# MLP up projection as Strassen products through DRAM, and the down projection as a phase of its own

## The chip, the cores and the metric

The kernel runs on one core of a Trainium2 chip. The metric is the device time of one execution in microseconds (us). The engines are PE (TensorE: matmuls and transposes), DVE (VectorE), ACT (ScalarE), POOL (GpSimd) and SP (SyncE, which here only issues DMAs). Each engine works through its own list of instructions in order.

## The reference

One encoder layer on 1024 tokens with a model width of 1024, and a final norm: windowed attention and a bidirectional SSD side by side, merged by gates, then cross attention, then the MLP with a hidden width of 4096. The change concerns the end:

```python
h = rmsnorm(x, norm_cross[i])
x = x + cross_attention(h, rmsnorm(mem, norm_mem[i]), w_xq[i], w_xkv[i], w_xo[i])
h = rmsnorm(x, norm_ffn[i])
x = x + jnp.square(jax.nn.relu(h @ w_up[i])) @ w_down[i]
return rmsnorm(x, norm_final)
```

All values are float32. A product is taken with each factor split in two parts, `hi` (rounded) and `lo` (the rest), and as three matmuls: hi by hi, hi by lo, lo by hi.

## The kernel before

A scheduler gives each engine its order from the program and from estimated durations; the order of the work is then fixed, and instructions wait on semaphores. Tiles come from pools in rotation: a tag has so many buffers, and who asks for the next waits until its last user is done.

`split_in` (L59 to L68) loads 128x1024 weights into `raw`, ACT writes their `hi` (L67) and POOL their `lo` (L68). `wload` gives it three buffers of each kind. `mm3` (L82, L86, L87) issues the three matmuls of a product. `gemm_fm` computes 128 hidden columns for 512 tokens: 8 slices of the width by 3 matmuls of 128x512. `norm_tile` (L130) norms 128 tokens (ACT L128, DVE L119, POOL L121, DVE L136), transposes them on PE (L141) and splits them into the tiles `kt` (ACT L144, DVE L145).

At the end of `merge_cross_phase` the cross attention's output projection, `xo_units`, adds 128x256 results (`xops`) into the eight residual tiles `x1` (L762), which stay in SBUF. For the second half of the tokens its four column groups alternate with the norms of the first half; the norms of the second half follow.

`mlp_phase` has 16 blocks of two hidden tiles of 128. `up` computes both tiles for both halves of the tokens into PSUM (`ups`, 96 matmuls in a block), forms relu(v) * v (ACT L822, DVE L824) and splits it (ACT L826, DVE L827) into `u`; it also loads the down weights (`wdh`, `wdl`). The down projection of a block adds, for eight token tiles and two column halves, six matmuls (`dps`) and one addition to `x1` (L850). The up projection of the next block is asked for ahead of the down projection of this one, so that both are mixed on PE. PSUM has four buffers of one bank (tag `p`: `xops`, `nt`, `dps`) and two of two banks (tag `g`: `ups`). The last block norms each token tile after its second addition and stores it (L854, L855).

## Time and profile before

| what | value |
|---|---|
| time, median of 3 runs (lowest to highest) | 2539.83 us (2535.67 to 2540.74) |
| span of the profiled execution | 2540.5 us |
| PE busy | 2446.7 us, 96% of the span |
| DVE, ACT, POOL busy | 1286.9, 1030.6, 936.2 us |
| matmuls of up and down projection | 1536 and 1536, of 128x512 |
| DMA traffic | 212.20 MB, 84 GB/s in the mean |

The span runs from the first to the last instruction of the profiled execution; that execution has no time of its own beside it, and the span lies 0.7 us over the median of the timed runs. Up and down projection take the last 700 us. "Busy" of PE counts matmuls that overlap in the array, so that a matmul's own duration is longer than the distance to the next one.

### The profile page before, as it was taken

What the parts mean: (1) busy time and instruction counts of PE and PEld (TensorE: products, weight loads), DVE (VectorE), ACT (ScalarE), POOL (GpSimd) and SP (SyncE); (2) the same over time, 40 slices, a digit from 0 to 9 for tenths busy, and PEclk for the clock granted to TensorE, in tenths of its full rate; (3) what the DMA queues carried; (4) which work ended last, traced back from release to release, by engine and by line L of the source; (5) the groups of instructions that cost most, each with busy time, mean ns of one, the idle gap of its engine ahead of it and who ended that gap; (6) DMA issues with size and microseconds to landing.
All of it is one profiled execution on the core that took longest, in us unless ns stands there. A gap on an engine that the chain in (4) does not pass through costs nothing.

```text
span 2540.5 us, 32272 instructions
## 1 busy us (share of the span) xinstructions
PE 2446.7 (96%) x12348; PEld 2014.4 (79%) x12348; DVE 1286.9 (51%) x2033; ACT 1030.6 (41%) x2114; POOL 936.2 (37%) x808
## 2 busy tenths in 40 slices
PE   7899999999999999999999999999999999999998
PEld 6677877777787778777778878888988888888887
DVE  5856556565755655465553342335543434343435
ACT  5445436363544534576773232235432121212112
POOL 4253434344344433444454444224332131312120
PEclk9999999999999999999999999999999999999999
DMA  6223223131313312111125454412121121111111
GB/s 221 75 71 104 92 59 117 52 123 46 112 63 88 108 44 90 48 48 46 50 90 201 134 206 129 170 50 67 59 75 67 34 67 34 66 34 58 42 34 67
DMA packets 135914, 212.20 MB, mean 84 GB/s; under 512 B 9680, under 2 KB 84560, under 8 KB 135760
## 3 DMA queue, kind: packets, MB, share of 16 engines
q1 hardware_dynamic: 58528, 159.80, 18.9%
q10 hardware_dynamic: 77232, 50.35, 6.7%
q8 instruction: 97, 1.59, 0.3%
q14 instruction: 57, 0.47, 0.1%
HBM read 183.63 MB, written 26.48 MB: 83 GB/s over the span
## 4 chain that ended last, share of the span: by engine, by line
PE 71%; DVE 12%; ACT 6%; POOL 4%; DMA 3%; issue 3%; ACTq 0%; POOLq 0%; SPq 0%; DVEq 0%
PE dps L87 4%; PE dps L86 4%; PE dps L82 4%; PE ups L82 4%; PE ups L86 4%; PE ups L87 4%; PE mps L87 3%; PE mps L82 3%; PE mps L86 3%; PE zp L82 2%; PE zp L87 2%; PE zp L86 2%; DMA rows<-d_cs 2%; PE st L373 2%; PE gps L82 2%
## 5 line engine op out<-in xcount | busy, mean ns | idle before, releaser
L68 POOL TENSOR_TENSOR wlo<-raw,whi 128x1024 fp32r<-128x1024 f32 x170 | 416.6, 2452 | 570.4 <-ACT whi L67 556.4
L67 ACT ACTIVATE whi<-raw 128x1024 fp32r<-128x1024 f32 x172 | 181.8, 1057 | 365.0 <-PE mps L86 111.7
L850 DVE TENSOR_TENSOR x<-x,dps 128x512 f32<-128x512 f32 x256 | 175.6, 686 | 124.9 <-PE dps L87 123.2
L68 POOL TENSOR_TENSOR wdl<-raw,wdh 128x1024 fp32r<-128x1024 f32 x32 | 76.0, 2396 | 423.2 <-ACT wdh L67 423.2
L82 PE MATMUL cps<-kt,whi 128*128 128x512 f32 x512 | 203.0, 396 | 6.9 <-DVE cx L334 6.9
L86 PE MATMUL cps<-kt,whi 128*128 128x512 f32 x512 | 203.8, 398 | 0.0
L87 PE MATMUL cps<-kt,wlo 128*128 128x512 f32 x512 | 201.4, 393 | 0.0
L82 PE MATMUL ups<-kt,whi 128*128 128x512 f32 x512 | 199.7, 390 | 0.2
L86 PE MATMUL ups<-kt,whi 128*128 128x512 f32 x512 | 199.4, 390 | 0.0
L87 PE MATMUL ups<-kt,wlo 128*128 128x512 f32 x512 | 199.2, 389 | 0.0
L86 PE MATMUL dps<-wdl,u 128*128 128x512 f32 x512 | 199.2, 389 | 0.0
L87 PE MATMUL dps<-wdh,u 128*128 128x512 f32 x512 | 199.2, 389 | 0.0
L82 PE MATMUL dps<-wdh,u 128*128 128x512 f32 x512 | 199.2, 389 | 0.0
L824 DVE TENSOR_TENSOR u<-ups,ru 128x512 f32<-128x512 f32 x64 | 44.1, 689 | 256.5 <-ACT ru L822 254.3
L67 ACT ACTIVATE wdh<-raw 128x1024 fp32r<-128x1024 f32 x32 | 32.3, 1053 | 229.9 <-PE dps L87 229.7
L82 PEld LDWEIGHTS cps<-kt,whi 128*128 128x128 f32 x512 | 96.6, 189 | 27.1 <-issue 7.7
L82 PEld LDWEIGHTS ups<-kt,whi 128*128 128x128 f32 x512 | 96.1, 188 | 20.7 <-DVE u L824 0.6
L86 PEld LDWEIGHTS ups<-kt,whi 128*128 128x128 f32 x512 | 96.1, 188 | 20.0 <-DVE kt L145 0.2
L87 PEld LDWEIGHTS ups<-kt,wlo 128*128 128x128 f32 x512 | 96.1, 188 | 20.0
L87 PEld LDWEIGHTS dps<-wdh,u 128*128 128x128 f32 x512 | 96.1, 188 | 20.0
L82 PEld LDWEIGHTS dps<-wdh,u 128*128 128x128 f32 x512 | 96.1, 188 | 20.0
L86 PEld LDWEIGHTS dps<-wdl,u 128*128 128x128 f32 x512 | 96.1, 188 | 19.9
(311 smaller groups left out, 6460.2 us busy)
## 6 DMA issues: line engine op xcount, KB each, us to landing
rows<-d_cs ACTq DMA_DIRECT2D x128, 256.0 KB, 3.8
raw<-in_wssd_dram SPq DMA_DIRECT2D x48, 512.0 KB, 3.9
raw<-in_wsb_dram SPq DMA_DIRECT2D x32, 512.0 KB, 3.3
raw<-in_wup_dram SPq DMA_DIRECT2D x32, 512.0 KB, 3.2
raw<-in_wdn_dram SPq DMA_DIRECT2D x32, 512.0 KB, 3.2
x<-in_x_dram SPq DMA_DIRECT2D x16, 512.0 KB, 7.7
raw<-in_wg_dram SPq DMA_DIRECT2D x16, 512.0 KB, 3.9
raw<-in_wa_dram SPq DMA_DIRECT2D x16, 512.0 KB, 3.3
```

Source lines behind the costliest of these rows:

```text
L67: nc.scalar.activation(hi, raw, AF.Copy)
L68: (eng or nc.gpsimd).tensor_tensor(lo, raw, hi.bitcast(F32), ALU.subtract)
L82: i = mm(out, l[0], r[0], start=first, stop=False)
L86: mm(out, l[0], r[1], start=False, stop=False)
L87: mm(out, l[1], r[0], start=False, stop=last)
L373: PE.matmul(st[:, lo:hi], btok[:, c], xs.rearrange("p d h q -> p (d h q)")[:, lo:hi], start=True, stop=True)
L824: V.tensor_tensor(u2, pv, r, ALU.mult)
L850: V.tensor_tensor(xh, xh, ps, ALU.add)
```

## The change

For each pair of hidden tiles and both halves of the tokens, the up projection is a 2 by 2 product of blocks (token halves by halves of the width, times halves of the width by hidden tiles). Before, it is computed as eight block products; after, as the seven of Strassen's scheme in Winograd's form. The four sums of activation blocks (s1 to s4) are formed once, in `Up.sums`, the sums of weight blocks in `Up.weights` for every pair; each operand of a product is split into `hi` and `lo` by `put` (ACT L887, POOL L888; L867 for the activations). The products add in PSUM where they can: `pb` takes products 1, 6, 7, 4 in turn, `pc` products 5 and 3, and between them ACT copies and DVE adds form the four results, square them and store them to DRAM (`d_u`, L924, L964).

`up_phase` begins with the second half's cross output, first for two of its four token tiles, between the norms of the first half; four residual tiles go to DRAM (`d_x`) and their space is closed. Then come the sums of the fifth and sixth token tile, the cross output of the other two tiles (its weights are loaded again), products 1 and 2 of the first two pairs, the last two sums, and 16 `quad`s. The down projection becomes `down_phase`, with pools of its own that open when all before it are closed: eight blocks of four hidden tiles, whose `u` is loaded and split again (ACT, DVE), with twelve matmuls in a PSUM group. `wload` takes both parts from one tag with six buffers.

```diff
...
-        hi = kx.wp.tile([P, 1024], F32R, tag="whi", bufs=kx.w_bufs, name="whi")[:, :n]
-        lo = kx.wp.tile([P, 1024], F32R, tag="wlo", bufs=kx.w_bufs, name="wlo")[:, :n]
+        hi = kx.wp.tile([P, 1024], F32R, tag="wop", bufs=6, name="whi")[:, :n]
+        lo = kx.wp.tile([P, 1024], F32R, tag="wop", bufs=6, name="wlo")[:, :n]
...
+        x1p = x1_open()
...
+            xt = x1p[t // 4].tile([P, D], F32, tag="x1", bufs=4, name="x1")
...
-        kx.h3T = [act_tiles(kx)]
-        for i in range(4):
-            xo_units(1, oks[1], i)
-            norm(0, i, g_ffn, kx.h3T)
-        kx.h3T.append(act_tiles(kx))
-        for i in range(4):
-            norm(1, i, g_ffn, kx.h3T)
...
-def mlp_phase(kx, ins, out):
+    return oks[1], g_ffn
+def xo_units(kx, ins, h, ok, c, js=range(4)):
+    w = wsplit(wload(kx, ins["wxo"][c]), 4)
+    for j in js:
+        ps = kx.pp.tile([P, 512], F32, tag="p", name="xops")[:, :256]
+        for k in range(4):
+            mm3(kx, ps, act_pair([ok], k, slice(j * P, (j + 1) * P)), w[k], k == 0, k == 3)
+        xh = kx.x1[4 * h + j][:, c * 256:(c + 1) * 256]
+        kx.nc.vector.tensor_tensor(xh, xh, ps, ALU.add)
+def up_phase(kx, ins, dr, ok, grow, x1_low):
+    nc, tc = kx.nc, kx.tc
+    with tc.tile_pool(name="p4", bufs=1, reuse_waits="tile") as mp:
+        a11, a12 = act_tiles(kx)
+        for c in range(4):
+            xo_units(kx, ins, 1, ok, c, (0, 1))
+            xn = mp.tile([P, D], F32, tag="ld", bufs=2, name="xn")
+            norm_tile(kx, mp, kx.x1[c], xn, grow, [a11, a12], c * P)
+            nc.sync.dma_start(dr.x1[c], kx.x1[c])
+        x1_low.close()
+        with tc.tile_pool(name="tp", bufs=1, side="right", reuse_waits="tile") as tp:
+            up = Up(kx, ins, dr, mp, tp, {"a11": a11, "a12": a12}, grow)
+            up.sums(0)
+            up.sums(1)
+            for c in range(4):
+                xo_units(kx, ins, 1, ok, c, (2, 3))
+            ws = [up.early_weights(b) for b in range(2)]
+            for b in range(2):
+                up.first(b, ws[b])
+            up.sums(2)
+            up.sums(3)
+            w = up.weights(0)
+            for b in range(16):
+                nxt = up.weights(b + 1) if b < 15 else None
+                up.quad(b, w)
+                w = nxt
+class Up:
+    LEFT = {1: "a11", 2: "a12", 3: "s4", 4: "a22", 5: "s1", 6: "s2", 7: "s3"}
+    def __init__(self, kx, ins, dr, mp, tp, s3, grow):
+        self.kx, self.ins, self.dr, self.mp, self.tp, self.s3, self.grow = kx, ins, dr, mp, tp, s3, grow
+        s3["s2"] = kx.mp.tile([P, 4, 2, 512], F32R, tag="kt", bufs=4, name="kt")
+        for key in ("s1", "a22", "s3", "s4"):
+            s3[key] = mp.tile([P, 4, 2, 512], F32R, tag=key, bufs=1, name=key)
+        self.early = {}
+    def t2(self, name):
+        return self.tp.tile([P, 512], F32, tag="t2", bufs=8, name=name)
+    def sums(self, i):
+        kx, s3 = self.kx, self.s3
+        nc = kx.nc
+        V, A, G, PE = nc.vector, nc.scalar, nc.gpsimd, nc.tensor
+        sl = slice(i * P, (i + 1) * P)
+        xt = kx.x1[4 + i]
+        xn = self.mp.tile([P, D], F32, tag="ld", bufs=2, name="xn")
+        r = norm_stats(kx, self.mp, xt, xn)
+        V.scalar_tensor_tensor(xn, xt, r[:, 0:1], self.grow, ALU.mult, ALU.mult)
+        pv = []
+        for kh in range(2):
+            ps = kx.pp.tile([P, 512], F32, tag="p", name="nt")
+            for j in range(4):
+                k = 4 * kh + j
+                PE.transpose(ps[:, j * P:(j + 1) * P], xn[:, k * P:(k + 1) * P], kx.ident)
+            pv.append(ps.rearrange("p (k c) -> p k c", k=4))
+        def hl(key):
+            return s3[key][:, :, 0, sl], s3[key][:, :, 1, sl]
+        def put(key, src, eng):
+            hi, lo = hl(key)
+            A.activation(hi, src, AF.Copy)
+            eng.tensor_tensor(lo, src, hi.bitcast(F32), ALU.subtract)
+        f1, f2, f3, f4 = (self.t2(n).rearrange("p (k c) -> p k c", k=4) for n in ("f1", "f2", "f3", "f4"))
+        h11, l11 = (x.bitcast(F32) for x in hl("a11"))
+        h12, l12 = (x.bitcast(F32) for x in hl("a12"))
+        A.activation(f1, pv[0], AF.Copy)
+        V.tensor_tensor(f3, h11, pv[0], ALU.subtract)
+        V.tensor_tensor(f1, f1, pv[1], ALU.add)
+        put("s1", f1, G)
+        V.tensor_tensor(f3, f3, l11, ALU.add)
+        V.tensor_tensor(f2, pv[1], f3, ALU.subtract)
+        put("s2", f2, G)
+        put("a22", pv[1], V)
+        put("s3", f3, G)
+        V.tensor_tensor(f4, h12, f2, ALU.subtract)
+        V.tensor_tensor(f4, f4, l12, ALU.add)
+        put("s4", f4, G)
+    def put(self, src):
+        t = self.kx.wp.tile([P, 2, 512], F32R, tag="wop", bufs=6, name="wop")
+        self.kx.nc.scalar.activation(t[:, 0], src, AF.Copy)
+        self.kx.nc.gpsimd.tensor_tensor(t[:, 1], src, t[:, 0].bitcast(F32), ALU.subtract)
+        return t
+    def raw(self, m):
+        r = self.kx.wp.tile([P, 1024], F32, tag="raw", bufs=self.kx.raw_bufs, name="raw")
+        self.kx.nc.sync.dma_start(r, self.ins["wup"][m])
+        return r[:, :512], r[:, 512:]
+    def weights(self, b):
+        V = self.kx.nc.vector
+        put = self.put
+        b11, b21 = self.raw(2 * b)
+        b12, b22 = self.raw(2 * b + 1)
+        ts = [self.t2(f"w{n}") for n in range(2)]
+        o = {} if b in self.early else {1: put(b11), 2: put(b21)}
+        V.tensor_tensor(ts[0], b12, b11, ALU.subtract)
+        V.tensor_tensor(ts[1], b22, ts[0], ALU.subtract)
+        o[6] = put(ts[1])
+        o[5] = put(ts[0])
+        V.tensor_tensor(ts[0], b22, b12, ALU.subtract)
+        o[7] = put(ts[0])
+        o[3] = put(b22)
+        V.tensor_tensor(ts[1], b21, ts[1], ALU.subtract)
+        o[4] = put(ts[1])
+        return o
+    def product(self, ps, w, n, start):
+        act = self.s3[self.LEFT[n]]
+        for k in range(4):
+            ks = slice(k * P, (k + 1) * P)
+            for m, (i, j) in enumerate(((0, 0), (0, 1), (1, 0))):
+                self.kx.nc.tensor.matmul(ps, w[:, i, ks], act[:, k, j], start=start and k == 0 and m == 0,
+                                         stop=k == 3 and m == 2, skip_group_check=True)
+    def square(self, c, b, j, h):
+        self.kx.nc.vector.scalar_tensor_tensor(c, c, 0.0, c, ALU.max, ALU.mult)
+        self.kx.nc.sync.dma_start(self.dr.u[2 * b + j][:, h * 512:(h + 1) * 512], c)
+    def early_weights(self, b):
+        b11, b21 = self.raw(2 * b)
+        return {1: self.put(b11), 2: self.put(b21)}
+    def first(self, b, w):
+        kx = self.kx
+        pb = kx.pp.tile([P, 512], F32, tag="p", name="pb")
+        cd = kx.pg.tile([P, S], F32, tag="g", name="pcd")
+        c11, c12 = self.t2("c11"), self.t2("c12")
+        self.product(pb, w[1], 1, True)
+        kx.nc.scalar.activation(c11, pb, AF.Copy)
+        self.product(cd[:, 512:], w[2], 2, True)
+        kx.nc.vector.tensor_tensor(c11, c11, cd[:, 512:], ALU.add)
+        self.square(c11, b, 0, 0)
+        self.early[b] = pb, cd, c12
+    def quad(self, b, w):
+        kx = self.kx
+        V, A = kx.nc.vector, kx.nc.scalar
+        if b not in self.early:
+            self.first(b, w)
+        pb, cd, c12 = self.early[b]
+        pc = cd[:, :512]
+        self.product(pb, w[6], 6, False)
+        A.activation(c12, pb, AF.Copy)
+        self.product(pc, w[5], 5, True)
+        c22, c21 = self.t2("c22"), self.t2("c21")
+        A.activation(c22, pc, AF.Copy)
+        self.product(pb, w[7], 7, False)
+        V.tensor_tensor(c22, c22, pb, ALU.add)
+        self.square(c22, b, 1, 1)
+        self.product(pc, w[3], 3, False)
+        V.tensor_tensor(c12, c12, pc, ALU.add)
+        self.square(c12, b, 1, 0)
+        self.product(pb, w[4], 4, False)
+        A.activation(c21, pb, AF.Relu)
+        A.activation(c21, c21, AF.Square)
+        kx.nc.sync.dma_start(self.dr.u[2 * b][:, 512:], c21)
+def down_phase(kx, ins, dr, out):
     nc, tc = kx.nc, kx.tc
     V, A, G, PE = nc.vector, nc.scalar, nc.gpsimd, nc.tensor
...
+    with tc.tile_pool(name="p6", bufs=1, reuse_waits="tile") as fp:
+        NB = 8
+        def block(b):
+            us, wd = [], []
+            for j in range(4):
+                m = 4 * b + j
+                raw = fp.tile([P, 1024], F32, tag="uraw", bufs=3, name="uraw")
+                nc.sync.dma_start(raw, dr.u[m])
+                ut = []
+                for h in range(2):
+                    t = fp.tile([P, 2, 512], F32R, tag="u", bufs=14, name="u")
+                    rh = raw[:, h * 512:(h + 1) * 512]
+                    A.activation(t[:, 0], rh, AF.Copy)
+                    V.tensor_tensor(t[:, 1], rh, t[:, 0].bitcast(F32), ALU.subtract)
+                    ut.append(t)
+                us.append(ut)
+                raw = fp.tile([P, 1024], F32, tag="draw", bufs=3, name="draw")
+                nc.sync.dma_start(raw, ins["wdn"][m])
+                hi = fp.tile([P, 1024], F32R, tag="wdh", bufs=7, name="wdh")
+                lo = fp.tile([P, 1024], F32R, tag="wdl", bufs=7, name="wdl")
+                A.activation(hi, raw, AF.Copy)
+                G.tensor_tensor(lo, raw, hi.bitcast(F32), ALU.subtract)
+                wd.append((hi, lo))
+            return us, wd
+        nxt = block(0)
+        for t in range(4):
+            kx.x1[t] = fp.tile([P, D], F32, tag="xl", bufs=4, name="xl")
+            nc.sync.dma_start(kx.x1[t], dr.x1[t])
...
         for b in range(NB):
             us, wd = nxt
             if b + 1 < NB:
-                nxt = up(b + 1)
+                nxt = block(b + 1)
             for t in range(NT):
                 for ch in range(2):
                     ps = kx.pp.tile([P, 512], F32, tag="p", name="dps")
                     cs = slice(ch * 512, (ch + 1) * 512)
-                    for j in range(2):
+                    for j in range(4):
                         mm3(kx, ps, kt_pair(us[j][t // 4], slice((t % 4) * P, (t % 4) * P + P)),
-                            (wd[j][0][:, cs], wd[j][1][:, cs]), j == 0, j == 1)
+                            (wd[j][0][:, cs], wd[j][1][:, cs]), j == 0, j == 3)
...
+    low = ctx.enter_context(ExitStack())
+    kx.wp = low.enter_context(tc.tile_pool(name="w", bufs=1))
+    kx.mp = low.enter_context(tc.tile_pool(name="m", bufs=1))
...
+        ok, grow = merge_cross_phase(kx, ins, dr, x1_open)
+        up_phase(kx, ins, dr, ok, grow, x1_low)
+    low.close()
+    down_phase(kx, ins, dr, out)
```

The order of the instructions moves at three places. The first is on PE at the end of the cross output. Before, the last norms' transposes (`nt`) lie directly ahead of the first up matmul:

```order
L141 MATMUL nt<-ident,xn 128x128 [waits DVE_49]
L141 MATMUL nt<-ident,xn 128x128 x3
L141 MATMUL nt<-ident,xn 128x128 [waits DVE_49]
L141 MATMUL nt<-ident,xn 128x128 x3
L82 MATMUL ups<-kt,whi 128x512 [waits Activation_49]
L86 MATMUL ups<-kt,whi 128x512 [waits DVE_49]
L87 MATMUL ups<-kt,wlo 128x512 [waits Pool_49]
```

After, the transposes of the first half's last tile (L141) and of the two sums (L858) come ahead of the cross output's last eight groups (`xops`):

```order
L141 MATMUL nt<-ident,xn 128x128 [waits DVE_49]
L141 MATMUL nt<-ident,xn 128x128 x3
L141 MATMUL nt<-ident,xn 128x128 [waits DVE_49]
L141 MATMUL nt<-ident,xn 128x128 x3
L858 MATMUL nt<-ident,xn 128x128 [waits DVE_49]
L858 MATMUL nt<-ident,xn 128x128 x7
L858 MATMUL nt<-ident,xn 128x128 [waits DVE_49,PE_49]
L858 MATMUL nt<-ident,xn 128x128 x3
L858 MATMUL nt<-ident,xn 128x128 [waits PE_49]
L858 MATMUL nt<-ident,xn 128x128 x3
L82 MATMUL xops<-whi,kt 128x256 [waits DVE_49]
L86 MATMUL xops<-wlo,kt 128x256 [waits Pool_49]
```

So in the changed kernel PE transposes three token tiles in one place, and cross output groups that need none of them stand behind.

The second place is on PE after products 1 and 2 of the first two pairs (`pcd` is product 2, `pb` product 6 of quad 0, the next `pcd` its product 5; `s_16142` is s1 and the `kt` of product 6 is s2):

```order
L919 MATMUL pcd<-kt,wop 128x512 [waits Pool_49]
L919 MATMUL pcd<-kt,wop 128x512 x9
L858 MATMUL nt<-ident,xn 128x128 [waits DVE_49]
L858 MATMUL nt<-ident,xn 128x128 x7
L858 MATMUL nt<-ident,xn 128x128 [waits DVE_49]
L858 MATMUL nt<-ident,xn 128x128 x3
L858 MATMUL nt<-ident,xn 128x128 [waits DVE_49,PE_49]
L858 MATMUL nt<-ident,xn 128x128 x3
L919 MATMUL pb<-kt,wop 128x512 [waits Activation_49]
L919 MATMUL pb<-kt,wop 128x512 [waits Pool_49] x2
L919 MATMUL pb<-kt,wop 128x512 x9
L919 MATMUL pcd<-s_16142,wop 128x512 [waits Activation_49]
```

There is nothing like it before: the transposes of the last two token tiles, each waiting for DVE, stand between the first products and the quads, and the first row of product 6 waits for ACT, the next for POOL.

On POOL the same place reads as follows (the low parts of s1, s3, s2 and s4 for two token tiles, then the weight of product 6):

```order
L867 TENSOR_TENSOR s_16142<-f_16458,s_16142 128x4x128 [waits Activation_49]
L867 TENSOR_TENSOR s_16144<-f_16460,s_16144 128x4x128 [waits Activation_49]
L867 TENSOR_TENSOR kt<-f_16459,kt 128x4x128 [waits Activation_49]
L867 TENSOR_TENSOR s_16145<-f_16461,s_16145 128x4x128 [waits Activation_49]
L867 TENSOR_TENSOR s_16144<-f_16499,s_16144 128x4x128 [waits Activation_49]
L867 TENSOR_TENSOR s_16142<-f_16497,s_16142 128x4x128 [waits Activation_49]
L867 TENSOR_TENSOR kt<-f_16498,kt 128x4x128 [waits Activation_49]
L867 TENSOR_TENSOR s_16145<-f_16500,s_16145 128x4x128 [waits Activation_49]
L888 TENSOR_TENSOR wop<-w_16523,wop 128x512 [waits PE_49,Activation_49]
```

The weight of product 6 is the ninth in the row; before, POOL splits only weights there.

The third is on SP between up and down projection. Before, loads of up and down weights alternate on its queue all through the MLP. After, the stores of the last quad (L924 the three that DVE finishes, L964 the one that ACT finishes) stand ahead of and between the first loads of the down phase (`uraw`, `draw`):

```order
L924 DMA d_u_162<-c_18515 128x512 [waits DMAHW2_49,DVE_49]
L924 DMA d_u_163<-c_18570 128x512 [waits DMAHW3_49,DVE_49]
L924 DMA d_u_163<-c_18516 128x512 [waits DMAHW4_49,DVE_49]
L978 DMA uraw<-d_u_132 128x1024 [waits DMAHW5_49,PE_49,Pool_49]
L964 DMA d_u_162<-c_18571 128x512 [waits DMAHW6_49,Activation_49]
L988 DMA draw<-in_wdn_dram 128x1024 [waits DMAHW7_49]
L978 DMA uraw<-d_u_133 128x1024 [waits DMAHW0_49]
L988 DMA draw<-in_wdn_dram 128x1024 [waits DMAHW1_49]
L978 DMA uraw<-d_u_134 128x1024 [waits DMAHW2_49,PE_49,Pool_49]
L988 DMA draw<-in_wdn_dram 128x1024 [waits DMAHW3_49]
L978 DMA uraw<-d_u_135 128x1024 [waits DMAHW5_49,DMAHW4_49,DVE_49]
L988 DMA draw<-in_wdn_dram 128x1024 [waits DMAHW7_49,Pool_49]
```

The first load of a down weight has moved from among the up projection's loads to behind the last store of the up phase.

More of the change, by code (lines that the diff above doesn't have):

```diff
@@ L224, in dt_part @@
     nc.sync.dma_start(raw, ins["wdt"])
-    w = kx.wp.tile([P, 1024], F32R, tag="whi", bufs=kx.w_bufs, name="wdt").rearrange("p (k s c) -> p k s c", k=8, s=2)
+    w = kx.wp.tile([P, 1024], F32R, tag="wop", bufs=6, name="wdt").rearrange("p (k s c) -> p k s c", k=8, s=2)
     rv = raw.rearrange("p (k c) -> p k c", k=8)
@@ L594, in attn_phase, with merge_cross_phase @@
                 gate_block(kx, ins, dr, m)
-def merge_cross_phase(kx, ins, dr, x1p_open):
+def merge_cross_phase(kx, ins, dr, x1_open):
     nc, tc = kx.nc, kx.tc
@@ L666, in merge_cross_phase @@
         wo = [load_wo(0, V)]
-        x1p = x1p_open()
         kx.x1 = []
+        x1p = x1_open()
         for t in range(NT):
-            xt = x1p.tile([P, D], F32, tag="x1", bufs=8, name="x1")
+            xt = x1p[t // 4].tile([P, D], F32, tag="x1", bufs=4, name="x1")
             nc.sync.dma_start(xt, ins["x"][t * P:(t + 1) * P])
@@ L753, in values @@
             V.tensor_tensor(ok[:, hd, 1], op, ok[:, hd, 0].bitcast(F32), ALU.subtract)
-        def xo_units(h, ok, c):
-            w = wsplit(wload(kx, ins["wxo"][c]), 4)
-            for j in range(4):
-                ps = kx.pp.tile([P, 512], F32, tag="p", name="xops")[:, :256]
-                for k in range(4):
-                    mm3(kx, ps, act_pair([ok], k, slice(j * P, (j + 1) * P)), w[k], k == 0, k == 3)
-                xh = kx.x1[4 * h + j][:, c * 256:(c + 1) * 256]
-                V.tensor_tensor(xh, xh, ps, ALU.add)
         for j in range(4):
@@ L851, in mlp_phase @@
                 if b == NB - 1:
-                    xn = fp.tile([P, D], F32, tag="u", bufs=8, name="xnf")
+                    xn = fp.tile([P, D], F32, tag="xnf", bufs=3, name="xnf")
                     r = norm_stats(kx, fp, kx.x1[t], xn)
@@ L879, in hybrid_encoder @@
     dr.gt = [[dp.tile([P, 512], F32, name=f"d_gt{k}_{h}") for h in range(2)] for k in range(16)]
+    dr.x1 = [dp.tile([P, D], F32, name=f"d_x{k}") for k in range(4)]
+    dr.u = [dp.tile([P, 1024], F32, name=f"d_u{k}") for k in range(32)]
     kx.dbg = dbg
```

38 lines of the change are left out of this document (5 added, 33 removed).

## The prediction

> **What bounds the kernel now.** I read the page first: busy time by engine, then the chain that ended last, then the costliest groups.
>
> ```profile
> span 2540.5 us, 32272 instructions
> PE 2446.7 (96%) x12348; PEld 2014.4 (79%) x12348; DVE 1286.9 (51%) x2033; ACT 1030.6 (41%) x2114; POOL 936.2 (37%) x808
> ...
> PE 71%; DVE 12%; ACT 6%; POOL 4%; DMA 3%; issue 3%; ACTq 0%; POOLq 0%; SPq 0%; DVEq 0%
> ...
> L82 PE MATMUL ups<-kt,whi 128*128 128x512 f32 x512 | 199.7, 390 | 0.2
> ```
>
> PE sets the time over the whole kernel, so each matmul taken out should count. But its price isn't the 390 ns of that last row: matmuls overlap. The next view cuts the span into stretches; its columns are length, then busy time and count of PE, PEld, DVE, ACT and POOL, then the granted clock, DMA share and GB/s.
>
> ```profile
> 1720.00:1750.00 30.00, 29.41 (x156) 25.21 (x155) 13.73 (x25) 14.09 (x36) 16.73 (x17) 1.00 0.23 77
> 1750.00:1780.00 30.00, 28.87 (x193) 25.55 (x192) 21.27 (x39) 19.77 (x53) 12.35 (x22) 1.00 0.11 37
> 1780.00:1840.00 60.00, 59.16 (x455) 56.19 (x453) 33.86 (x62) 26.57 (x43) 21.72 (x15) 1.00 0.19 62
> 1840.00:1900.00 60.00, 59.71 (x265) 48.72 (x264) 27.44 (x35) 17.94 (x26) 19.08 (x8) 1.00 0.24 80
> 1900.00:2000.00 100.00, 100.00 (x443) 82.78 (x442) 34.83 (x50) 21.17 (x28) 26.22 (x11) 1.00 0.16 54
> ```
>
> In the MLP (1900 to 2000 us) PE never stops, at full clock, and issues 443 matmuls in 100 us: **0.2257 us each**. A sum by 390 ns would be too large by a factor of 1.73. Of the way there, cross attention's output and the norms (1720 to 1900 us), PE loses only 0.59 + 1.13 + 0.84 + 0.29 = 2.85 us. Every new idle microsecond of PE in these stretches is therefore paid in full, since nothing there is slack.
>
> **The change part by part.** *Matmuls removed.* Before, a pair of hidden tiles takes 2 tiles x 2 halves x 8 k x 3 = 96 matmuls of 128x512; after, seven products x 4 k x 3 = 84. Sixteen pairs: 192 fewer, 192 x 0.2257 = **43.3 us** less. The down projection keeps its 1536 matmuls, the cross output its 384, the transposes their number. This is the whole gain; everything else costs or is hidden.
>
> *The steady quads.* A quad lasts 84 x 0.2257 = 19.0 us on PE, a product 2.71 us. What the other engines do in it has these nearest rows:
>
> ```profile
> L662 POOL TENSOR_TENSOR wo<-raw,wo 128x512 fp32r<-128x512 f32 x8 | 10.1, 1291 | 24.6 <-ACT wo L661 24.6
> L826 ACT ACTIVATE u<-u 128x512 fp32r<-128x512 f32 x64 | 40.5, 633 | 73.6 <-DVE u L824 73.6
> L822 ACT ACTIVATE ru<-ups 128x512 f32<-128x512 f32 x64 | 37.4, 584 | 93.5 <-PE ups L87 93.5
> L824 DVE TENSOR_TENSOR u<-ups,ru 128x512 f32<-128x512 f32 x64 | 44.1, 689 | 256.5 <-ACT ru L822 254.3 <-DVE u L827 0.5
> ```
>
> Seven weight splits cost POOL 7 x 1.29 = 9.0 us. ACT has seven splits at 0.63 and five copies or squares at 0.58, 7.3 us. DVE has ten operations at 0.69, 6.9 us. All are under 19.0. The tight place is ACT: after a product it must copy the result out of PSUM, 0.58, behind at most one split, 0.63, and PE needs that bank again one product later; 2.71 - 1.21 leaves about 1.3 us with the semaphores. So I cost the steady state at nothing: the next product hides the copies, and six operand buffers hide the splits. [...] The four stores of 256 KB and two loads of 512 KB in 19 us are small beside the DMA rate that follows; nothing waits for them.
>
> *First gap: the sums of the first two tiles.* Before, the cross output's last groups and the norms were interleaved so that little was lost. After, PE's order has the transposes of the fifth and sixth token tile ahead of the cross output's groups for the other two. A transpose waits for the whole norm, whose chain the last tile of the kernel shows (start, duration, operation):
>
> ```profile
> 2532.72 0.68 DVE L850 TENSOR_TENSOR x<-x,dps 128x512 f32<-128x512 f32 x1
> ...
> 2533.48 1.06 ACT L128 ACTIVATE xnf<-x 128x1024 f32<-128x1024 f32 x1 [1.51 <-issue]
> ...
> 2535.61 1.28 DVE L854 SCALAR_TENSOR_TENSOR xnf<-x,rr,gf 128x1024 f32<-128x1024 f32 x1 [0.73 <-POOL rr L121]
> ```
>
> The residual addition ends at 2533.40 and the normed tile is there at 2536.89: 3.5 us. The add of a cross output group is 0.42 and its norm's scaling 1.45 instead of 1.28:
>
> ```profile
> L136 DVE SCALAR_TENSOR_TENSOR xn<-x,rr,grow 128x1024 f32<-128x1024 f32 x26 | 37.6, 1447 | 19.0 <-POOL rr L121 19.0
> L762 DVE TENSOR_TENSOR x<-x,xops 128x256 f32<-128x256 f32 x32 | 13.0, 416 | 11.8 <-PE xops L87 11.7
> ```
>
> That makes 4.1 us to the fifth tile, 1.45 more to the sixth, then the transposes, and the next groups need PSUM buffers that ACT and DVE free only after a copy (0.58) and one to six operations of 0.69. Below stands about 6 us (the fifth tile's 4.1, the sixth's 1.45, the copy), above 11 (with all six operations and a norm operation held behind a POOL split of 2.4). I take **8.5**, by the chain with half of the six operations.
>
> *Second gap: the sums of the last two tiles.* After products 1 and 2 of the first two quads PE transposes the seventh and eighth tile, and the next product, number 6 of quad 0, needs the sum s2 of both and its weight's low part. POOL's order there has eight activation splits and then that weight: 9 x 1.29 = 11.6 us, after a copy, an addition and a split on ACT (0.58 + 0.69 + 0.63); about 2 us of transposes lie beside it. So 12 us, if DVE and POOL don't hold each other up. But these rows show that they do:
>
> ```profile
> 1864.78 2.40 POOL L68 TENSOR_TENSOR wlo<-raw,whi 128x1024 fp32r<-128x1024 f32 x1 [2.12 <-ACT whi L67]
> ...
> 1865.26 2.47 DVE L827 TENSOR_TENSOR u<-u,u 128x512 fp32r<-128x512 f32 x1 [4.93 <-ACT u L826]
> ...
> 1867.83 0.69 DVE L824 TENSOR_TENSOR u<-ups,ru 128x512 f32<-128x512 f32 x1
> ```
>
> L827 reads two SBUF operands and takes 2.47 us where L824, with one in PSUM, takes 0.69: it ends 0.55 us after POOL's operation does. Among the DVE work of this gap are eight operations of the kind of L827 (six in the sums, two weight differences), and POOL's chain needs most of their results. If each shifts the chain by its 0.69, 5.5 us are added: 12 to 18, and I take **16**, because the chain needs six of the eight. [...]
>
> *Third gap: from up to down.* The down phase has pools of its own in space that the up phase frees. On SP's queue its first load stands behind the store of the last quad's c12, about 1 us ahead of PE's last up product, and its first weight load behind the store of c21, which follows Relu and Square: 1.2 us after. A lone load lands in 3.2 us, and a full queue moves 399 GB/s, 1.3 us for 512 KB:
>
> ```profile
> raw<-in_wdn_dram SPq DMA_DIRECT2D x32, 512.0 KB, 3.2
> ...
> 5.00:10.00 5.00, 1.97 (x8) 1.57 (x8) 1.81 (x4) 2.72 (x5) 1.11 (x2) 1.00 0.99 399
> ...
> L67 ACT ACTIVATE wdh<-raw 128x1024 fp32r<-128x1024 f32 x32 | 32.3, 1053 | 229.9 <-PE dps L87 229.7
> L68 POOL TENSOR_TENSOR wdl<-raw,wdh 128x1024 fp32r<-128x1024 f32 x32 | 76.0, 2396 | 423.2 <-ACT wdh L67 423.2
> ```
>
> The weight lands at 1.2 + 3.2 = 4.4 us, its high part is there at 5.5, its low parts at 5.5 + 4 x 2.4 = 15.1 for the four tiles, and PE has only four PSUM groups to work on meanwhile, 48 x 0.2257 = 10.8 us, of which the last few wait for the fourth low part. That is at least 6 us idle. DVE's low parts of u read SBUF alone too, and eight of them (5.5 us) push the chain to 12. I take **10**, nearer the upper end since each of the four tiles has both.
>
> *Cold clock.* These three gaps are as long as two that the trace has:
>
> ```profile
> 99.88 0.77 PE L82 MATMUL cps<-kt,whi 128*128 128x512 f32 x1 [4.96 <-DVE cx L334]
> 100.00:103.00 3.00, 3.00 (x8) 2.35 (x8) 2.88 (x5) 2.35 (x3) 0.00 (x0) 0.50 0.04 10
> ...
> 1486.14 0.79 PE L87 MATMUL mps<-yk,wlo 128*128 128x512 f32 x1 [4.21 <-POOL wlo L68]
> 1488.00:1492.00 4.00, 4.00 (x11) 3.11 (x10) 0.00 (x0) 1.06 (x1) 1.81 (x2) 0.50 0.57 198
> ```
>
> After 4.96 us the granted clock is 0.50 for about 3 us, after 4.21 for about 6 (to 1492): at half pace that loses 1.4 and 2.8 us. Three gaps lose 3 to 6, and I take **4**. [...]
>
> *Hidden.* Loading the cross output's weights a second time, the spill and reload of four residual tiles (by the queue's rate, 1.3 us each), the down phase's 128 instead of 256 additions: all beside PE. The tail after the last matmul keeps its chain. The merged weight tag turns some orders in the SSD and attention stages; I bound that by -3 and +3 us and take nothing.
>
> *The sum.* -43.3 - 1.4 (half of the 2.85 us that PE loses there now, between none and all) + 8.5 + 16 + 10 + 4 = **-6.2 us**. From the profiled span, 2540.5, that is 2534.3; the median of the runs, 2539.83, lies 0.7 under that span, so I predict **2533.6 us**. By the low ends of the gaps it is -43.3 - 2.9 + 6 + 12 + 6 + 3 = -19, by the high ends -43.3 + 11 + 18 + 12 + 6 = +4; with 3 us for the earlier stages, 2518 to 2547.
>
> **The rivals.** *Gaps half covered.* The norms of the seventh and eighth tile can run beside products 1 and 2 (11 us), and the additions of the sums may fit between POOL's operations. With gaps of 6, 8, 5 and 2 us of cold clock the sum is -43.3 - 1.4 + 21 = -24: 2516 us. For it: DVE and ACT are free for most of that stretch. Against: POOL's nine operations depend on transposes that PE does only after those products.
>
> [...]
>
> *The count doesn't tell.* If a matmul cost 0.39 us the gain would be 75 us and the time 2502. The windows with 443 in 100 us speak against it so clearly that I give it no chance of its own. If products that add to a bank begun earlier ran slower than the up projection's, the gain would shrink; its matmuls have the same shape and already add to one bank 24 times, so none either.
>
> **How the numbers follow.** The forecast's case has 0.62, the half-covered gaps 0.18, the wait in each quad 0.20. A measurement of this kernel can tell about 0.2%, 5.1 us, from no change, so faster means under 2534.7. The forecast lies just beyond that line: of its 0.62 I put 0.36 on faster, 0.24 within, 0.02 on slower. The half-covered case is all faster; of the quad's wait 0.17 are slower and 0.03 within. Together 0.54, 0.27, 0.19. The range 2515 to 2551 holds the forecast's bounds, the half-covered case and the mildest part of the waits, leaving out about 0.2.
>
> **What would show it.** The seven products of a quad at 18.9 to 19.1 us, PE without idle time inside it, prove the gain; idle time before products 7, 5 or 3 with ACT as releaser proves the wait. One idle stretch of 6 to 11 us before the cross output's last groups, one of 12 to 18 before product 6 of quad 0, released by POOL, one or several of 6 to 12 after the last up product, and a clock of 0.50 after each, prove the costs. The prediction is wrong if the three gaps together are under 25 us or over 50, or if the stages ahead of the MLP move by more than 3 us.

## The result and the profile after

The changed kernel takes 2595.95 us (median of 4 runs, 2590.45 to 2603.07) against 2537.75 before (4 runs): a ratio of 1.0232 with a 95% interval of 1.0201 to 1.0263. It is slower by 58 us, where 6.2 us less were forecast, and lies far above the forecast's range of 2515 to 2551.

The page of the profiled execution after, which is the longest of its four runs, begins with these lines:

```profile
span 2601.1 us, 32506 instructions
PE 2442.4 (94%) x12156; PEld 2001.6 (77%) x12156; DVE 1343.2 (52%) x2021; ACT 1087.6 (42%) x2230; POOL 1059.1 (41%) x908
```

The span is 60.6 us longer while PE is busy for 4.3 us less. A good place to cut the span is the first matmul of the cross output (`xops`), since all that the change rewrote comes behind it. Its row in the view of one tile (count: shortest, median and longest duration, first and last start), before:

```profile
L82 PE MATMUL xops<-whi,kt x128: 278/283/387, 1770.1 to 1828.8; 128*128 128x256 f32 x128
```

and after:

```profile
L82 PE MATMUL xops<-whi,kt x128: 278/283/562, 1801.1 to 1879.6; 128*128 128x256 f32 x128
```

So 31.0 us of the 60.6 are lost **ahead** of the rewritten part, in code that the diff leaves alone but for the tag of its weight buffers, and 29.6 from that matmul on (800.1 against 770.4 us to the end; I call this stretch the rest).

**Where the first 31 us are.** The view of what PE waits for (total, times, longest) after, then before:

```profile
PE yt L454 <- ACT yz L450: 36.7, 16, 3.6
...
PE pcd L919 <- DVE c L939: 10.4, 13, 1.0
...
PE pb L919 <- ACT wop L887: 8.3, 1, 8.3
PE dps L82 <- ACT wdh L991: 8.3, 1, 8.3
```

```profile
PE yt L454 <- ACT yz L450: 18.8, 16, 2.3
```

In the SSD stage each group of heads ends in transposes (`yt`) that wait for ACT; these waits doubled, and the longest went from 2.3 to 3.6 us. One of them in the trace after, with what POOL did ahead of it (start, duration, operation, idle time before and its cause), and the windows around it (columns as in the prediction; the last three are granted clock, DMA share and GB/s):

```profile
636.73 0.64 POOL L413 TENSOR_SCALAR_AFFINE_SELECT rows<-rows 128x512 f32<-128x512 f32 x1 [3.36 <-DMA rows<-d_cs]
637.33 0.61 POOL L439 TENSOR_TENSOR p<-xtok,dsk 128x256 f32<-128x256 f32 x1
...
646.81 0.69 PE L454 MATMUL yt<-ident,yz 128*128 128x128 f32 x2 [3.62 <-ACT yz L450]
...
648.58 1.91 PE L431 MATMUL yo<-prev,cC 128*128 128x512 f32 x2
...
643.00:647.00 4.00, 0.38 (x2) 0.19 (x2) 1.49 (x3) 2.36 (x8) 2.01 (x2) 0.82 0.00 0
647.00:652.00 5.00, 5.00 (x19) 3.86 (x19) 1.98 (x3) 2.09 (x6) 0.70 (x2) 0.50 0.29 58
```

The same place before:

```profile
618.32 0.74 POOL L413 TENSOR_SCALAR_AFFINE_SELECT rows<-rows 128x512 f32<-128x512 f32 x1 [1.57 <-DMA rows<-d_cs]
...
627.98 0.44 PE L454 MATMUL yt<-ident,yz 128*128 128x128 f32 x2 [0.97 <-ACT yz L450]
...
628.00:632.00 4.00, 4.00 (x26) 3.19 (x27) 2.40 (x4) 3.11 (x8) 0.98 (x3) 1.00 0.22 66
```

POOL waits 3.36 us (before: 1.57) for a load of `rows`, and the product (L439) that the group's last sums need stands behind that wait. At the end of that chain PE idles 3.62 us (before: 0.97) and **runs the next 5 us at half clock**, a granted clock of 0.50, where before the clock stayed at 1.00. Between 63 and 1060 us the trace records 4 such stretches before and 14 after; half of PE's busy time in them is 6.7 us before and 27.9 after. That is 21 us more, and idle time adds 72.4 - 60.7 = 11.7: together 33, which is the 31 within the way they are counted. So idle time is the smaller part; longer waits are followed by half clock more often. After, the three waits of `yt` over 3.2 us are each followed by 6.8 us at half clock, and of the twelve between 1.6 and 3.0 us six by 3.4; before, none of its eleven waits of 0.9 to 2.3 us is.

**The rewritten part.** A quad in the steady state, after:

```profile
2031.19 2.88 PE L919 MATMUL pb<-kt,wop 128*128 128x512 f32 x12
...
2031.86 0.69 DVE L903 TENSOR_TENSOR w<-raw 128x512 f32<-128x512 f32 x1 [6.86 <-DMA raw<-in_wup_dram]
2032.15 1.55 POOL L888 TENSOR_TENSOR wop<-raw,wop 128x512 fp32r<-128x512 f32 x1 [1.42 <-ACT wop L887]
2032.59 1.66 DVE L904 TENSOR_TENSOR w<-raw,w 128x512 f32<-128x512 f32 x1
2034.17 0.67 DVE L939 TENSOR_TENSOR c<-c,pcd 128x512 f32<-128x512 f32 x1
...
2034.90 3.05 PE L919 MATMUL pcd<-s,wop 128*128 128x512 f32 x12 [0.82 <-DVE c L939]
...
2037.78 2.96 PE L919 MATMUL pb<-s,wop 128*128 128x512 f32 x12
...
2040.58 2.95 PE L919 MATMUL pcd<-s,wop 128*128 128x512 f32 x12
...
2046.15 2.89 PE L919 MATMUL pb<-kt,wop 128*128 128x512 f32 x12
...
2048.87 2.88 PE L919 MATMUL pcd<-kt,wop 128*128 128x512 f32 x12
```

Two things show. Product 5 (`pcd<-s`, 2034.90) waits for L939, the addition that reads product 2 out of the other half of the same PSUM tile; L939 stands on DVE behind two weight differences, the first waiting for its load and the second taking 1.66 us instead of 0.69 while POOL splits a weight (L888, 2032.15 to 2033.70); it ends 0.55 us after POOL's operation, as L827 does in the prediction's rows. And products with `kt` follow each other after 2.72 us (2046.15 to 2048.87), those with `s` after 2.80 (2037.78 to 2040.58). The distance from one matmul to the next, the pitch, is 233 ns there and not 226.6. A quad takes 20.4 us instead of 19.0.

The second and the third gap, after, with the rows of DVE, ACT and POOL that end the longest wait of the second one:

```profile
1893.45 0.66 PE L858 MATMUL nt<-ident,xn 128*128 128x128 f32 x4 [1.53 <-DVE f L873]
1898.96 1.09 PE L858 MATMUL nt<-ident,xn 128*128 128x128 f32 x4 [4.86 <-DVE a L867]
1905.87 1.15 DVE L882 TENSOR_TENSOR f<-f,kt 128x512 f32<-128x512 f32 x1
1907.05 0.63 ACT L866 ACTIVATE s<-f 128x512 fp32r<-128x512 f32 x1 [3.58 <-DVE f L882]
1907.65 1.15 ACT L887 ACTIVATE wop<-w 128x512 fp32r<-128x512 f32 x2
1907.76 1.28 POOL L867 TENSOR_TENSOR s<-f,s 128x512 fp32r<-128x512 f32 x1 [1.29 <-ACT s L866]
1908.33 1.22 PE L919 MATMUL pb<-kt,wop 128*128 128x512 f32 x2 [8.28 <-ACT wop L887]
1910.32 4.64 PE L919 MATMUL pb<-kt,wop 128*128 128x512 f32 x10 [0.76 <-POOL wop L888]
...
2237.39 1.22 PE L82 MATMUL dps<-wdh,u 128*128 128x512 f32 x2 [8.28 <-ACT wdh L991]
2239.82 0.80 PE L86 MATMUL dps<-wdl,u 128*128 128x512 f32 x1 [1.22 <-POOL wdl L992]
```

Ten matmuls at 1910.32 take 4.64 us, where twelve take 2.88 at 2031.19. PE's wait of 8.28 us ends with ACT's high part of the weight of product 6 (L887), which stands behind a split that waits for DVE's last sum (L882); POOL's low part of that weight adds the 0.76. In the down phase the view of waits has one more row:

```profile
PE dps L82 <- DVE xl L1014: 2.1, 6, 0.4
```

At the start of six blocks PE waits for the last additions of the block before. From the last matmul ahead of such a wait to the third behind it are 1.31 us (2295.16 to 2296.47), where three pitches of 0.2266 are 0.68: some 0.62 us a block, 3.7 us in all.

The account of the rest, in us, each term from the starts in the trace:

| term | forecast | measured | how |
|---|---|---|---|
| 192 matmuls fewer | -43.3 | -43.5 | at 0.2266 |
| first gap and its half clock | +9.8 | +17.3 | first `xops` to product 1 of quad 0: 78.9; the same work before took 60.7, and 8 transposes more are 0.9 |
| second gap | +17.3 | +24.2 | two quads from 1880.0 to 1944.1, less 2 x 19.03 and 1.8 for 16 transposes |
| steady quads | 0 | +18.3 | 14 quads in 284.8, less 14 x 19.03 |
| third gap and the down phase | +11.3 | +16.0 | last product's end at 2228.9 to the last `dps`' at 2593.0, less 1536 x 0.2266 |
| waits that were there before | -1.4 | -2.9 | |
| ahead of the first `xops` | 0 | +31.0 | |
| sum | -6.2 | +60.4 | spans differ by 60.6 |

(The forecast's 4 us of half clock are shared equally among the gaps.)

### The profile page after: what moved, and what is told of

Same layout as the page of the kernel before. It is cut to its first block, busy times and chain, and to the rows that moved or that the text cites. A ratio compares the mean times of both kernels' runs of the same rounds, so it can differ in the third digit from the quotient of the medians.

```text
span 2601.1 us, 32506 instructions
## 1 busy us (share of the span) xinstructions
PE 2442.4 (94%) x12156; PEld 2001.6 (77%) x12156; DVE 1343.2 (52%) x2021; ACT 1087.6 (42%) x2230; POOL 1059.1 (41%) x908
## 3 DMA queue, kind: packets, MB, share of 16 engines
q8 instruction: 96, 1.57, 0.2%
## 5 line engine op out<-in xcount | busy, mean ns | idle before, releaser
L68 POOL TENSOR_TENSOR wlo<-raw,whi 128x1024 fp32r<-128x1024 f32 x142 | 347.9, 2451 | 530.1 <-ACT whi L67 505.6
L992 POOL TENSOR_TENSOR wdl<-draw,wdh 128x1024 fp32r<-128x1024 f32 x32 | 85.5, 2696 | 251.2 <-ACT wdh L991 251.1
L888 POOL TENSOR_TENSOR wop<-w,wop 128x512 fp32r<-128x512 f32 x64 | 95.2, 1489 | 103.2 <-ACT wop L887 98.9
L82 PEld LDWEIGHTS cps<-kt,whi 128*128 128x128 f32 x512 | 97.8, 191 | 26.5 <-issue 6.9
L423 ACT ACTIVATE eb<-rows,ebias 128x128 f32<-128x128 f32 x256 | 94.0, 390 | 54.3 <-POOL rows L415 54.0
L87 PEld LDWEIGHTS cps<-kt,wlo 128*128 128x128 f32 x512 | 97.8, 191 | 19.0
L86 PEld LDWEIGHTS cps<-kt,whi 128*128 128x128 f32 x512 | 97.7, 191 | 19.0
L86 PE MATMUL gps<-kt,whi 128*128 128x512 f32 x256 | 110.1, 430 | 0.0
L422 ACT ACTIVATE ef<-rows,ebias 128x128 f32<-128x128 f32 x256 | 92.6, 390 | 40.5 <-POOL rows L413 30.6
L82 PE MATMUL gps<-kt,whi 128*128 128x512 f32 x256 | 107.8, 421 | 0.0
L984 DVE TENSOR_TENSOR u<-uraw,u 128x512 fp32r<-128x512 f32 x64 | 98.5, 1574 | 15.3 <-ACT u L983 15.3
L919 PE MATMUL pcd<-s,wop 128*128 128x512 f32 x384 | 96.2, 399 | 10.4 <-DVE c L939 10.4
```

The source lines that it names most:

```text
L68: (eng or nc.gpsimd).tensor_tensor(lo, raw, hi.bitcast(F32), ALU.subtract)
L82: i = mm(out, l[0], r[0], start=first, stop=False)
L86: mm(out, l[0], r[1], start=False, stop=False)
L87: mm(out, l[1], r[0], start=False, stop=last)
L422: A.activation(ef[:, h], rows[:, 0, h], AF.Exp, bias=kx.ebias[:, b, j, 0, 4 * g + h:4 * g + h + 1])
L423: A.activation(eb[:, h], rows[:, 1, h], AF.Exp, bias=kx.ebias[:, b, j, 1, 4 * g + h:4 * g + h + 1])
```

## The experiments

Since the stage ahead of `xops` differs by several us between executions of one kernel (half-clock stretches come and go), two numbers stand for each kernel: the ratio of its time to that of the kernel before, with a 95% interval, and the rest, which that stage doesn't touch but which is known from the one profiled execution alone.

**1. Two tags again, in the changed kernel.** Weights go to `whi` and `wlo` as before the change, and the products' operands take the two tags in turn; every engine has the order of the kernel before up to the end of cross attention.

```diff
-        hi = kx.wp.tile([P, 1024], F32R, tag="wop", bufs=6, name="whi")[:, :n]
-        lo = kx.wp.tile([P, 1024], F32R, tag="wop", bufs=6, name="wlo")[:, :n]
+        hi = kx.wp.tile([P, 1024], F32R, tag="whi", bufs=kx.w_bufs, name="whi")[:, :n]
+        lo = kx.wp.tile([P, 1024], F32R, tag="wlo", bufs=kx.w_bufs, name="wlo")[:, :n]
...
-        t = self.kx.wp.tile([P, 2, 512], F32R, tag="wop", bufs=6, name="wop")
+        self.n = 1 - self.n
+        t = self.kx.wp.tile([P, 2, 512], F32R, tag=("whi", "wlo")[self.n], bufs=self.kx.w_bufs, name="wop")
```

> The changed kernel with the two weight tags of the kernel before (three buffers for hi, three for lo; the products' operands take them in turn), which gives every engine the order of the kernel before up to the end of cross attention. Theory: the one tag reordered the SSD stage, and that costs 31 us of the 58; the first xops matmul comes at about 1770 us again, not 1801, the waits of yt for ACT fall from 36.7 to about 19 us, and the time is about 2565 us. Rival (the SSD stage is slower for another reason, such as the pools or the tensors in DRAM, or by the run): first xops still at about 1800, time about 2596.

Measured: 2566.91 us, ratio 1.0118 (1.0093 to 1.0143); first `xops` at 1771.7, rest 802.5.

**2. One tag in the kernel before**, and nothing else.

> The kernel before with nothing changed but the one tag of six weight buffers. Theory: the SSD stage takes the changed kernel's order and its 31 us: first xops at about 1801 us, time about 2569 us. Rival: the tag costs nothing by itself and the time stays at 2538 us within 5.

Measured: 2566.03 us, ratio 1.0118 (1.0099 to 1.0137). The waits of `yt` in the two, experiment 1 first, then 2:

```profile
PE yt L454 <- ACT yz L450: 18.4, 16, 2.3
```

```profile
PE yt L454 <- ACT yz L450: 36.1, 16, 3.4
```

The tag alone moves the waits and 28 to 29 us from one kernel to the other, in both directions: the theory holds, and its rivals don't. The profiled execution of experiment 2 was one of its short ones, with 9 half-clock stretches in the SSD stage and not 14, and its first `xops` came at 1786.0. Its order up to there is that of the changed kernel, and PE's idle time ahead of that matmul is nearly the same (96.2 against 98.6 us), so that most of the 15 us between the two is the clock. Its rest is 770.2, that of the kernel before. What in the scheduler's sums turns its choice when the tag changes was not traced, nor was the way from the order to each longer wait, but for the one shown above.

**3 and 4. The pitch, and product 5's wait**, each on top of experiment 1. Experiment 3 pads the sum tiles to a multiple of 512 bytes; experiment 4 takes product 5 and 3 out of product 2's tile:

```diff
+        mp.tile([P, 32], F32, name="pad")
         for key in ("s1", "a22", "s3", "s4"):
...
-        pc = cd[:, :512]
+        pc = kx.pp.tile([P, 512], F32, tag="p", name="pc")
```

> The kernel e1_tags_apart with 128 bytes of padding ahead of the tiles s1, a22, s3 and s4, so that they start at a multiple of 512 bytes as the kt tiles do; the order is the same. Theory: products 3, 4, 5 and 7 go at a pitch of 233 ns and not 226.6 because their moving operand starts 384 bytes past such a multiple; here the pitch is 226 to 227 for all seven, 768 x 6.5 ns = 5 us less than e1_tags_apart. Rival (their address above 128 KB, or the turn between two banks, is what slows them): the pitch stays at 233 and the time at that of e1_tags_apart.

> The kernel e1_tags_apart with products 5 and 3 in a PSUM tile of their own in place of half of product 2's tile. Theory: product 5 waits about 0.8 us in each quad for the addition of product 2 (L939), which shares its tile and stands on DVE behind two weight differences; with a tile of its own that wait is gone, a quad takes 19.3 us and not 20.4, and the time is 13 to 16 us under e1_tags_apart. Rival (DVE is late in any case and PE meets it at product 7 or 4): idle time moves to those products, and the time stays within 5 us of e1_tags_apart.

The same 200 us of the steady quads in experiments 1, 3 and 4, in this order (length, PE's busy time and count, ...):

```profile
1950.00:2150.00 200.00, 191.60 (x822) 153.39 (x820) 83.00 (x100) 68.68 (x118) 101.69 (x70) 1.00 0.32 104
```

```profile
1950.00:2150.00 200.00, 191.10 (x831) 154.89 (x830) 82.37 (x98) 69.47 (x119) 103.01 (x70) 1.00 0.32 105
```

```profile
1950.00:2150.00 200.00, 200.00 (x869) 162.83 (x869) 79.29 (x103) 71.83 (x123) 106.68 (x73) 1.00 0.33 110
```

Matmuls in the same time are the plainest measure: 822, 831, 869. With its own tile PE never stops; DVE's addition still starts some 2.8 us behind product 2, as in experiment 1, and nothing waits for it. The rest falls from 802.5 to 786.3, the 16 us expected. The ratio is 1.0077 (1.0052 to 1.0101), and the median, 2557.99, falls by 8.9 us only; as the four runs of experiment 1 spread over 14 us, the size rests on the traces. Alignment gives the pitch back (226.6 in all seven products, a quad in 20.20 us and not 20.44, so 4 us in sixteen), but the rest is only 2 us shorter and the median, 2566.90, unchanged: a gain of this size is under what these runs tell.

**5. Both.**

> e3_aligned and e4_own_bank together: two weight tags, aligned sum tiles, own PSUM tile for products 5 and 3. Theory: the two costs are independent, so a quad takes 19.0 to 19.1 us, that is 84 x 0.2266, the stretch from product 1 of quad 0 to the first dps matmul about 339 us (343.4 in e4_own_bank less 4 to 5), time about 2552 us. What is left over the kernel before is then the three gaps and the cold clock behind them. Rival (the two hide each other): the stretch stays at 343.

Measured: 2551.59 us, ratio 1.0066 (1.0045 to 1.0087), rest 784.6.

```profile
1900.00:2100.00 200.00, 200.00 (x884) 165.64 (x884) 79.42 (x105) 74.30 (x127) 109.07 (x74) 1.00 0.34 113
```

884 matmuls in 200 us, 0.226 us each: the steady quads now run as the prediction had them. What is left is the gaps.

**6. Other work in the gaps.**

```diff
+            for c in range(2):
+                xo_units(kx, ins, 1, ok, c, (2, 3))
             up.sums(0)
             up.sums(1)
-            for c in range(4):
+            for c in range(2, 4):
...
-            for b in range(2):
-                up.first(b, ws[b])
+            up.first(0, ws[0])
             up.sums(2)
             up.sums(3)
+            up.first(1, ws[1])
...
-        kx.nc.sync.dma_start(self.dr.u[2 * b][:, 512:], c21)
+        kx.nc.scalar.dma_start(self.dr.u[2 * b][:, 512:], c21)
```

> e5_both with three edits, one for each gap: half of the cross output's last groups ahead of the fifth and sixth tile's sums; the seventh and eighth tile's sums between the first products of quad 0 and quad 1 and not behind both; the store of c21 issued by ACT, so that SP's queue goes straight on to the loads of the down phase. Theory: the gaps are waits of PE for work that starts too late, and other matmuls can stand in them: the first gap loses 6 to 8 of its 12 us, the second 4 to 6 of its 18, the third 2 of its 8; with less half clock behind them 12 to 18 us in all, time about 2537 us, level with the kernel before. Rival (POOL's and DVE's chain sets the end of the first two gaps whatever PE does, since they only start when the last cross output is there): the idle time moves behind the moved matmuls and the time falls by less than 5 us.

Measured: 2542.65 us, ratio 1.0020 (1.0008 to 1.0031), rest 774.1: 10.5 us less than in experiment 5, a little under what was expected (median 8.9 us less).

**7. Matmuls that only keep PE busy**, in experiment 6's gaps; 54 are added, and their results aren't used.

```diff
+            warm(kx, up.early[0][1][:, :512], a11, 34)
...
+            warm(kx, kx.pg.tile([P, S], F32, tag="g", name="warm")[:, :512], up.s3["s4"], 20)
...
+def warm(kx, ps, t, n):
+    for _ in range(n):
+        i = kx.nc.tensor.matmul(ps, t[:, 0, 0, :P], t[:, 0, 0], start=True, stop=True)
+        kx.tc.keep_in_program_order(i)
```

> e6_short_gaps with matmuls that compute nothing that is used, put into PE's idle time: 34 of 128x512 between products 1 and 2 of quad 1 and the first product that needs a sum, 20 between the last up product and the first dps. Theory: part of each gap's cost is the half clock behind it (stretches of 13.7 and 10.2 us at 0.50 in e6_short_gaps); if PE stays busy the clock stays at 1.0 there, the gaps keep their ends, and the time falls by 6 to 10 us, to 2533 to 2537 us, level with the kernel before or just under it. Rival (the clock follows something other than PE's idle time, or the added matmuls delay the work behind them): the stretches at 0.50 stay, or the 54 matmuls add up to 12 us.

The second and third gap in experiment 6 and then in 7, by windows:

```profile
1862.00:1876.00 14.00, 7.77 (x17) 5.19 (x18) 8.40 (x9) 3.68 (x6) 9.83 (x7) 0.51 0.27 94
2169.00:2179.00 10.00, 5.50 (x12) 3.92 (x13) 6.78 (x6) 7.53 (x11) 5.95 (x3) 0.53 1.01 402
```

```profile
1859.00:1870.00 11.00, 10.86 (x48) 8.43 (x46) 10.79 (x13) 5.62 (x11) 10.87 (x8) 1.00 0.00 1
1870.00:1880.00 10.00, 6.43 (x15) 4.35 (x16) 6.41 (x4) 2.82 (x5) 8.41 (x6) 0.68 0.34 123
2171.00:2181.00 10.00, 7.29 (x31) 5.37 (x30) 4.04 (x5) 6.53 (x10) 3.42 (x2) 1.00 1.02 375
```

Where PE is kept busy the clock stays at 1.00 in this execution, which agrees with the theory that the clock follows PE's idle time. Behind the second gap it still falls to half for 6.8 us, where waits remain (0.60, 2.61 and 0.50 us). The rest is 770.9, 3.2 us less; median 2539.83, ratio 1.0012 (1.0000 to 1.0023). The gain is half of the lower end expected, and the intervals of experiments 6 and 7 overlap, so that the times don't show it. Nor did the clock hold every time: experiments 8, 9 and 11 keep the 20 matmuls of the third gap, and each of their profiled executions has 6.8 us at half clock there, as here in experiment 8:

```profile
2169.00:2179.00 10.00, 7.28 (x18) 5.51 (x19) 7.97 (x5) 7.60 (x10) 8.20 (x4) 0.66 1.02 417
```

The waits behind those 20 matmuls are hardly longer there (1.05 to 1.37 and 1.70 to 1.71 us) than in experiment 7 (1.01 and 1.70), so the length of a wait alone doesn't decide.

**8. Two of the four sums split on DVE** instead of POOL.

```diff
-        put("s2", f2, G)
+        put("s2", f2, V)
...
-        put("s4", f4, G)
+        put("s4", f4, V)
```

> e7_warm with the low parts of s2 and s4 written by DVE in place of POOL. Theory: the second gap ends when POOL has done nine splits of 1.29 us in a row; with five left on POOL and four at 0.69 on DVE it ends 2 to 4 us earlier, and so does the kernel. [...]

Measured: 2540.81 us, ratio 1.0011 (1.0000 to 1.0023), rest 773.4. The time can't be told from experiment 7's, and the rest, 2.5 us longer, has the half clock in the third gap that experiment 7 lacks (3.0 us); the scheduler also turned the order of the first products. Inconclusive.

**9. A third pair's first products in the second gap**, in place of 34 of the unused matmuls; the first two pairs keep products 1 and 2 in one two-bank tile each.

> e7_warm with products 1 and 2 of a third pair in the second gap in place of the 34 unused matmuls; the first two pairs hold their products 1 and 2 in one two-bank PSUM tile each, so that the third has buffers. Theory: the gap's ends are set by the sums, so 24 matmuls that have to be done anyway stand in time that was idle: 24 x 0.2266 = 5.4 us less, time about 2534 us, 0.1% under the kernel before. Rival (PSUM buffers or the six operand buffers hold something up in turn): time within 2 us of e7_warm, with a new wait in the first three quads.

Measured: 2538.62 us, ratio 1.0002 (0.9989 to 1.0015), rest 770.9, the same as in experiment 7. This is what the rival has, and new waits show in that stretch:

```profile
1840.04 4.61 PE L932 MATMUL pcd<-kt,wop 128*128 128x512 f32 x12 [1.77 <-ACT c L955]
...
1856.19 2.98 PE L932 MATMUL pd<-kt,wop 128*128 128x512 f32 x12 [2.12 <-DVE a L879]
1860.79 3.06 PE L932 MATMUL pcd<-kt,wop 128*128 128x512 f32 x12 [1.62 <-ACT c L955]
```

Product 2 now shares a tile with product 1 and waits for ACT's copy of it (L955), the trouble of experiment 4 made anew. These two waits are 3.4 of the 5.4 us that were expected; where the rest stays was not traced.

**10. Alignment by itself, in the kernel before**: 480 bytes of padding behind the tiles `at` of the merge stage. Their pool lies at the upper end of the space (`side="right"`), so padding behind them moves their start down to a multiple of 512.

```diff
+                if h == 0:
+                    atp.tile([P, 120], F32, name="pad")
```

> The kernel before with 480 bytes of padding behind the tiles at, which are the moving operand of 384 matmuls in the merge stage and start 480 bytes past a multiple of 512; the order is the same. Theory (a moving operand off such a multiple costs 3%): the pitch of mps<-at falls from 232 to 236 ns to 226 to 228, 384 x 7 ns = 2.7 us less, time 0.1% under the kernel before, at the edge of what can be told. Rival (only the new sum tiles were concerned, for another reason): the pitch stays.

The row of one of their matmuls in the kernel before, then in this one:

```profile
L82 PE MATMUL mps<-at,whi x128: 395/396/397, 1338.2 to 1598.1; 128*128 128x512 f32 x128
```

```profile
L82 PE MATMUL mps<-at,whi x128: 388/389/390, 1332.8 to 1589.9; 128*128 128x512 f32 x128
```

All 128 are 7 ns shorter, and sixteen runs of 24 matmuls take 5.21 us and not 5.37. The time, 2535.81 us, ratio 0.9990 (0.9978 to 1.0002), can't be told from no change.

**11. Experiments 9 and 10 together.**

> e9_three_early and e10_at_aligned together. Theory: both gains add, time about 2531 to 2532 us, 0.2% under the kernel before. Rival: the spread of the clock's stretches in the SSD stage, some 5 us between executions, covers the difference.

Measured: 2536.00 us, ratio 0.9993 (0.9981 to 1.0004), rest 770.2. Level with the kernel before: no version here beats it clearly.

## Why the prediction was wrong, point by point

*The saving* was right: 84 matmuls at 0.2266 us a quad, -43.5 us, and experiment 5 runs at that rate.

*"The merged weight tag turns some orders in the SSD and attention stages; I bound that by -3 and +3 us"* is the largest failure: 31 us in the profiled executions, 28 to 29 between the medians (experiments 1 and 2). The orders had been seen to differ, but were priced without asking which waits they touch. The row that spoke was there: the waits of `yt` for ACT were the longest in total on PE, up to 2.3 us each, and the prediction's own rows said that the clock drops after some length of idling up to 4.2 us, but not from which. The trace of before had shorter ones too: of its eight waits of `st` over 1.6 us three (1.89, 2.34 and 1.88 us, ended at 235.2, 345.0 and 461.2) are followed by 3.4 us at 0.50. A little more, up to 3.6 us, was enough.

*"So I cost the steady state at nothing"* failed by 18.3 us in the 14 quads. The wait in each quad, to which I gave 0.20 as my own estimate and ACT as the releaser, is there (0.82 us in the quad shown), but its releaser is DVE's addition of product 2, some 2.8 us behind that product, which PE meets only because the tile is shared. ACT's slack of 1.3 us held. About 14 us are this wait (experiment 4), and the other 4 to 5 are a term that the sum lacked altogether, the pitch of an operand that starts off a multiple of 512 bytes (233 ns and not 226.6, experiments 3 and 10). It was readable in the trace of before: `mps<-at` at 396 ns against 389 for `mps<-yk`.

*The first gap* was set at 8.5 us from the two sums alone. Their waits, and those of the groups behind them, are 8.2 us (3.1, 3.5, 0.5 and 1.1), so that term holds. But the stretch measured 17.3: the norms of the first half already lost time before it (idle 1.0, 0.5, 1.4 and 1.6 us), because only 24 matmuls stand between them where 48 did, a moved part whose old cover I didn't count, and the half clock took 2.9.

*The second and third gap* came out near in idle time, 17.65 us against 16 and 9.5 against 10, but not wholly for the reasons given, which is partly luck. In the second, POOL and DVE do hold each other up (DVE's sums take up to 1.7 us and not 0.69, POOL's splits up to 1.72 and not 1.29), but I expected POOL as the releaser; it was ACT behind DVE's sums that ended the wait of 8.28 us, and POOL's low part the 0.76 after it. In the third I had the first weight's high part at 5.5 us and the rest of the idle time from POOL's low parts; PE waited 8.28 us for the high part, since its load, issued at 2230.85 as one of several, was there for ACT only at 2236.28, not after 3.2 us, and then only 1.22 us for the first low part. What brought the two terms to 24.2 and 16.0 us is mainly the half clock (5.3 and 2.2 us) and, in the down phase, the six waits for DVE's additions (3.7 us), which the sum didn't have.

*The cold clock* was put at 4 us for three gaps. The rest has 10.4 us of it (half of PE's busy time in its stretches at 0.50), the kernel before none. The rows gave 1.4 and 2.8 us for one gap, but a gap here is a row of waits, and the clock stays down over all of them (20.5 us at 0.50 from 1894.9 on, around the second gap). The stretches at 0.50 that end within the spans of before and after last 3.4, 6.8, 10.2 and 20.5 us, so that one of 3.4 us with PE busy throughout costs 1.7 us. The 4 us that I took, less than one such stretch for each gap, were too little.

*DVE's operations on SBUF alone* take longer beside POOL's in the steady quads too (L904, 1.66 us against 0.69). In the quad shown, the 0.97 us that this adds are more than the 0.82 for which product 5 waits, but the load that the difference before it waits for makes DVE late too, and the two were not told apart. I had weighed such delays in the gaps (2.47 us against 0.69), not in DVE's way to product 2.
